# A one-layer bidirectional hybrid encoder: the norm factor broadcast as a stationary operand, and the last products and stores shared out differently

## The chip, the cores and the metric

One Trainium2 chip, one of its cores. A core has five engines with a queue each: TensorE (PE, matrix products), VectorE (DVE), ScalarE (ACT), GpSimd (POOL) and SyncE (SP, which here only issues DMAs; ACT's queue issues some as well). The metric is the device time of one execution in microseconds, as a median of several executions; lower is better. Everything is float32, one sequence of 512 tokens, 1024 channels.

## The reference

```python
def _rmsnorm(x, w):
    xf = x.astype(jnp.float32)
    y = xf * lax.rsqrt(jnp.mean(xf * xf, axis=-1, keepdims=True) + EPS)
    return (y * w.astype(jnp.float32)).astype(x.dtype)

def _modulate(x, shift, scale):
    return x * (1.0 + scale) + shift

def reference(x, c, ...):
    h = x
    c_act = jax.nn.silu(c)
    mod = c_act @ w_ada + b_ada
    sh1, sc1, g1, sh2, sc2, g2, sh3, sc3, g3 = jnp.split(mod, 9, axis=-1)
    u = _modulate(_rmsnorm(h, norm_ffn1), sh1, sc1)
    h = h + 0.5 * g1 * _swiglu(u, w_ffn1_up, w_ffn1_down)
    u = _modulate(_rmsnorm(h, norm_mix), sh2, sc2)
    h = h + g2 * _hybrid_mixer(u, ...)
    u = _modulate(_rmsnorm(h, norm_ffn2), sh3, sc3)
    h = h + 0.5 * g3 * _swiglu(u, w_ffn2_up, w_ffn2_down)
    return _rmsnorm(h, norm_final)
```

The two feed-forward nets have 2816 inner channels. The mixer projects `u` to 7712 columns, and has a gated short convolution (branch A) and a bidirectional gated DeltaNet of 8 heads (branch B): five-tap convolutions of q, k and v, per-head decays, a chunked delta-rule scan in each direction, a gated norm. Both branches are projected, merged by gates and projected once more. What this change touches is the RMSNorm: four times the factor `rsqrt(mean(x*x) + EPS)` of each token is needed on all channels, and the last time the result is the output.

## The kernel before

Channels lie on the 128 partitions and tokens along the rows: `h` is 8 tiles of 128 x 512. A weight tile of 512 KB is loaded by SP (L167, tile `raw`), split into two exact parts by ACT (L172, `hi`) and DVE (L174, `lo`), and each product is three matmuls, L184 to L186. PE does these nearly all the time.

The sum over channels for a norm crosses partitions, so PE does it: the squares are summed over the tiles on DVE (L208), and `rstd_bcast` (L211 to L233) multiplies them as the stationary operand by a column of ones (L218, L221), which gives 128 sums, one per partition and token. DVE turns them into means (L223, `ms`), POOL raises them to the power -1/2 (L226, `rs`, one column for every 128 tokens). To bring the factor of a token onto all partitions, DVE makes a diagonal matrix of each column (L229, `diag`), and PE multiplies ones by it (L232): each row of the result holds the factors of all tokens. The function runs seven times: once for 512 tokens at the start (into the PSUM bank `kq`), and at the end of each feed-forward net and of the mixer twice, for the tokens 0 to 255 (`kq`) and 256 to 511 (`o`). Those six come from `residual` (L251), which gives the last product tile in two halves of the tokens, adds the residual (L256) and starts what follows on the first half.

At the start (L887 to L925) DVE computes the modulation from `w_ada` by products with an accumulator (L147, output `junk`), and each tile of `h` times the factor (L913 on DVE, L911 on POOL) goes through ACT (L915) to `u` and PE (L917). At the end `final` (L968 to L973) multiplies each tile of `h` by its norm weight and the factor, one DVE instruction per tile (L970), and stores tiles in pairs, alternately by SP's and ACT's queue (L973).

In the mixer eight heads are built one after the other. A head's decays come back from DRAM as `Gb` (L467), 128 x 8 x 128 on every partition, in a single buffer: the next head's load waits for this head's last readers (L526). DVE reads it at L512 and L514, ACT takes exponentials (L515), and DVE forms `ef` and `eb` (L526). Then PE multiplies k by k and q (L545, L546), and DVE scales the results (L550, L554). ACT's L482 takes sums of squares of what PE has transposed (L477).

The order of tasks in the mixer comes from a hand-written list, EMIT. Beyond that, the instructions of each engine stand in an order that a scheduler makes from the program's order, priorities (`high_priority`) and its own costs. Each engine then runs its queue strictly in that order, waiting wherever an operand or a buffer is missing. So a changed instruction can move others far away from it.

## Time and profile before

| What | Value |
|---|---|
| Median of 3 runs | 1392.18 us (1391.95 to 1394.26) |
| Profiled execution, span | 1388.2 us |
| PE busy | 1342.6 us, 97% |
| DVE busy | 824.8 us, 59% |
| ACT busy | 565.6 us, 41% |
| POOL busy | 71.9 us, 5% |
| Last matmul of the down products starts | 1376.26 us |
| Last store is issued | 1384.6 us |

Of the profiled execution only the span, first to last instruction, is known; the times of the runs are some 4 us above it. A line of the timeline reads: start in us, duration, engine, line of the program, operation, output and inputs, shapes, count, and in brackets the time that the engine was idle before it with what it waited for last. A row such as "PE acc L917 <- ACT u L915: 6.9, 6, 2.2" says who waited for whom: total us, how often, the longest. A row that begins with two times and a colon is a stretch: its length, the busy time (and count) of PE, of PE's weight loads, of DVE, ACT and POOL, the granted clock of PE as a share of full speed, the busy share of the DMA engines and GB/s. SPq and ACTq are DMA issues on these queues.

### The profile page before, as it was taken

How to read it: one execution, taken by the hardware profiler on the slowest of the kernel's cores; microseconds unless marked ns; L12 is line 12 of the kernel's file. 1: busy time of each engine (PE TensorE's matmuls, PEld its weight loads, DVE VectorE, ACT ScalarE, POOL GpSimd, SP SyncE). 2: the span in 40 equal slices, each digit the busy share in tenths (PEclk: the TensorE clock that was granted, in tenths of full speed). 3: DMA queues.
4: the chain of work that ended last, by engine and by line, in shares of the span. 5: the costliest groups of instructions: out<-in, count | busy, mean ns of one | idle time of the engine just before them, and what ended most of it. 6: DMA issues, size and time to landing. Idle time of an engine off the chain costs nothing.

```text
span 1388.2 us, 19980 instructions
## 1 busy us (share of the span) xinstructions
PE 1342.6 (97%) x7359; PEld 1101.4 (79%) x7359; DVE 824.8 (59%) x2199; ACT 565.6 (41%) x1156; POOL 71.9 (5%) x109
## 2 busy tenths in 40 slices
PE   5999999999999999999999999999999999999997
PEld 2588888888897777878787787888898888888886
DVE  7856655655566778787764784647653444443343
ACT  3433333322346654467645333545433333332230
POOL 2000000000010110021112001000000000000000
PEclk9999999999999999999999999999999999999998
DMA  8655555645532446334342333567503333332331
GB/s 278 220 173 182 177 188 167 193 158 190 173 126 71 123 122 154 125 92 131 113 139 73 113 112 100 161 197 253 177 31 106 122 112 131 122 115 86 99 110 61
DMA packets 88131, 193.50 MB, mean 139 GB/s; under 512 B 24737, under 2 KB 37217, under 8 KB 87906
## 3 DMA queue, kind: packets, MB, share of 16 engines
q1 hardware_dynamic: 72400, 163.77, 38.1%
q10 hardware_dynamic: 15634, 28.46, 5.9%
q8 instruction: 58, 0.95, 0.3%
q14 instruction: 39, 0.32, 0.1%
HBM read 171.19 MB, written 21.00 MB: 138 GB/s over the span
## 4 chain that ended last, share of the span: by engine, by line
PE 80%; DMA 7%; DVE 6%; issue 4%; ACT 3%; POOL 1%; ACTq 0%; POOLq 0%; DVEq 0%; SPq 0%
PE acc L186 23%; PE acc L185 23%; PE acc L184 23%; DMA Gb<-grow 2%; DMA msb<-gtd 2%; DVE junk L147 1%; DVE lo L174 1%; PE ch L672 1%; DMA raw<-w_o 1%; PE ch L683 1%; PE o L695 1%; PE tp L477 1%; PE tp L608 1%; PE ch L700 1%; ACT hi L172 1%
## 5 line engine op out<-in xcount | busy, mean ns | idle before, releaser
L185 PE MATMUL acc<-uh,lo 128*128 128x512 f32 (+1 forms) x1256 | 486.2, 387 | 1.3 <-DVE lo L174 1.3
L184 PE MATMUL acc<-uh,hi 128*128 128x512 f32 (+1 forms) x1256 | 486.4, 387 | 0.7 <-ACT hi L172 0.6
L186 PE MATMUL acc<-ul,hi 128*128 128x512 f32 (+1 forms) x1256 | 485.2, 387 | 0.0
L172 ACT CAST hi<-raw 128x512 fp32r<-128x512 f32 (+1 forms) x424 | 257.5, 613 | 540.4 <-PE acc L186 481.5
L174 DVE TENSOR_TENSOR lo<-raw,hi 128x512 fp32r<-128x512 f32 (+1 forms) x424 | 286.4, 681 | 282.7 <-ACT hi L172 281.5
L185 PEld LDWEIGHTS acc<-uh,lo 128*128 128x128 f32 x1256 | 237.3, 189 | 44.5 <-DVE lo L174 1.8
L184 PEld LDWEIGHTS acc<-uh,hi 128*128 128x128 f32 x1256 | 237.2, 189 | 44.4 <-ACT hi L172 1.0
L186 PEld LDWEIGHTS acc<-ul,hi 128*128 128x128 f32 x1256 | 236.9, 189 | 42.7
L147 DVE SCALAR_TENSOR_TENSOR junk<-raw,cs 128x256 f32<-128x256 f32 x288 | 111.3, 437 | 60.3 <-DMA raw<-w_ada 60.1
L184 PE MATMUL acc<-gh,hi 128*128 128x512 f32 (+1 forms) x396 | 145.1, 366 | 0.0
L186 PE MATMUL acc<-gl,hi 128*128 128x512 f32 (+1 forms) x396 | 145.1, 366 | 0.0
L185 PE MATMUL acc<-gh,lo 128*128 128x512 f32 (+1 forms) x396 | 144.7, 365 | 0.0
L184 PEld LDWEIGHTS acc<-gh,hi 128*128 128x128 f32 x396 | 74.7, 189 | 12.2
L185 PEld LDWEIGHTS acc<-gh,lo 128*128 128x128 f32 x396 | 74.7, 189 | 12.0
L186 PEld LDWEIGHTS acc<-gl,hi 128*128 128x128 f32 x396 | 74.7, 189 | 12.0
L442 DVE SCALAR_TENSOR_TENSOR cacc<-acc,cvd_sb,cacc 128x510 f32<-128x510 f32 (+1 forms) x96 | 71.1, 743 | 7.5 <-ACT cacc L437 6.9
L311 DVE TENSOR_TENSOR sa<-sa,acc 128x512 f32<-128x512 f32 x42 | 28.8, 686 | 35.3 <-PE acc L186 35.3
L226 POOL TENSOR_TENSOR rs<-ms,mhalf 128x2 f32<-128x2 f32 (+1 forms) x7 | 5.7, 813 | 830.4 <-DVE ms L223 817.5
L194 ACT CAST gh<-sa 128x512 fp32r<-128x512 f32 x44 | 27.4, 622 | 23.7 <-DVE sa L311 18.5
L204 ACT ACTIVATE sq<-h 128x512 f32<-128x512 f32 (+1 forms) x25 | 14.1, 563 | 46.5 <-DVE h L256 46.3
L195 DVE TENSOR_TENSOR gl<-sa,gh 128x512 fp32r<-128x512 f32 x44 | 30.5, 692 | 3.3 <-ACT gh L194 1.4
L917 PE MATMUL acc<-u,lw 128*128 128x512 f32 x48 | 25.3, 667 | 6.9 <-ACT u L915 6.9
(242 smaller groups left out, 1399.5 us busy)
## 6 DMA issues: line engine op xcount, KB each, us to landing
raw<-w_ada SPq DMA_DIRECT2D x72, 512.0 KB
raw<-w_in SPq DMA_DIRECT2D x60, 512.0 KB
raw<-w2u SPq DMA_DIRECT2D x44, 512.0 KB
raw<-w1u SPq DMA_DIRECT2D x40, 512.0 KB
raw<-w1d SPq DMA_DIRECT2D x16, 512.0 KB
raw<-w2d SPq DMA_DIRECT2D x16, 512.0 KB
Gb<-grow SPq DMA_DIRECT2D x8, 512.0 KB
dl<-nl SPq DMA_DIRECT2D x8, 512.0 KB
```

What stands on the lines that cost most here:

```text
L147: dve.scalar_tensor_tensor(out=junk[:], in0=raw[:, q, :], scalar=1.0, in1=cs[:, q, :], op0=ALU.mult, op1=ALU.mult, accum_out=part[:, n, q ...
L172: act.copy(hi[:], raw[:, k : k + n, :])
L174: dve.tensor_sub(lo[:], raw[:, k : k + n, :], hi[:].bitcast(F32))
L184: pe.matmul(ps[:, t0:t1], wh, rh[:, k0 + k, t0:t1], start=a, stop=False)
L185: pe.matmul(ps[:, t0:t1], wl, rh[:, k0 + k, t0:t1], start=False, stop=False)
L186: pe.matmul(ps[:, t0:t1], wh, rl[:, k0 + k, t0:t1], start=False, stop=b)
L194: act.copy(hi, src)
L195: dve.tensor_sub(lo, src, hi.bitcast(F32))
L204: act.activation(out=sq[:], in_=hk, func=ACT.Square)
L311: dve.tensor_mul(sa[:], sa[:], ps[1][:])
L442: dve.scalar_tensor_tensor(out=acc[:, lo:hi], in0=src[:, lo + o : hi + o], scalar=w[:, i : i + 1], in1=acc[:, lo:hi], op0=ALU.mult, op1=AL ...
L917: pe.matmul(early[m][:], lw[:, m, k, :], u0[:], start=k == 0, stop=k == KT - 1)
```

## The change

In `rstd_bcast` the diagonal matrices are gone, and so is the product of ones with them. For each 128 tokens PE multiplies with a stationary operand that is the column `rs` repeated 128 times (read with a stride of zero) and the identity as the moving operand: the result holds again the factors of all tokens on each partition. DVE has sixteen instructions less, and PE has n matmuls of 128 columns in place of one of n x 128.

In `final`, for tokens 256 to 511 only, ACT copies the factor from PSUM to SBUF (`bs`); for tiles 0, 1 and 2 ACT multiplies `h` by the norm weight, which needs no factor, and POOL multiplies the result by `bs`; the other five tiles go through DVE as before. Each tile is stored by itself, tiles 0, 2, 4 and 6 by SP's queue, the others by ACT's. The first half of the tokens is treated as before.

```diff
     def rstd_bcast(sums, t0, t1, tag):
...
         rs = sm["p"].tile([P, NC], F32, tag="rs", name="rs")
         pool.tensor_tensor(out=rs[:, 0:n], in0=ms[:, 0:n], in1=mhalf[:, 0:n], op=ALU.pow)
-        diag = sm["p"].tile([P, n, P], F32, tag="sq", name="diag")
+        bc = bank(tag, psx)
         for i in range(n):
-            dve.tensor_scalar(out=diag[:, i, :], in0=ident[:], scalar1=rs[:, i : i + 1], scalar2=None,
-                              op0=ALU.mult)
-        bc = bank(tag, psx)
-        pe.matmul(bc[:, 0 : t1 - t0], ones[:], diag[:].rearrange("p a b -> p (a b)"), start=True, stop=True)
+            pe.matmul(bc[:, i * P : i * P + P], rs[:, i : i + 1].to_broadcast([P, P]), ident[:], start=True, stop=True)
         return bc
...
     def final(t0, t1, bc):
+        n = t1 - t0
+        some = (0, 1, 2) if t1 == T else ()
+        if some:
+            bs = sm["p"].tile([P, n], F32, tag="bs", bufs=1, name="bs")
+            act.copy(bs[:], bc[:, 0:n])
         for k in range(KT):
-            dve.scalar_tensor_tensor(out=h[:, k, t0:t1], in0=h[:, k, t0:t1], scalar=nw[:, 3, k : k + 1],
-                                     in1=bc[:, 0 : t1 - t0], op0=ALU.mult, op1=ALU.mult)
-            if k % 2:
+            hk = h[:, k, t0:t1]
+            if k in some:
+                act.activation(out=hk, in_=hk, func=ACT.Copy, scale=nw[:, 3, k : k + 1])
+                pool.tensor_tensor(out=hk, in0=hk, in1=bs[:], op=ALU.mult)
+            else:
+                dve.scalar_tensor_tensor(out=hk, in0=hk, scalar=nw[:, 3, k : k + 1], in1=bc[:, 0:n], op0=ALU.mult,
+                                         op1=ALU.mult)
+            if some:
+                (nc.sync, nc.scalar)[k % 2].dma_start(out[:, k, t0:t1], hk)
+            elif k % 2:
                 (nc.sync, nc.scalar)[k // 2 % 2].dma_start(out[:, k - 1 : k + 1, t0:t1], h[:, k - 1 : k + 1, t0:t1])
```

The scheduler gives another order, above all at the start, at the boundary to the mixer and in the mixer. Three places are shown; lines of the new kernel stand some four lower in the mixer (L463 there is L467 above, L508 is L512, L510 is L514, L438 is L442, L546 is L550, L550 is L554, L562 is L566, L568 is L572).

SP's DMA issues in the mixer around the load of `Gb` for the fourth head, before (`dl` and `A` are the way of the inverses' blocks to DRAM and back, `raw` a weight tile):

```order
L566 DMA dl<-nl 128x1024
L572 DMA A<-dl 8x32x32
L167 DMA raw<-w_in 128x1024
L572 DMA A<-dl 8x32x32 x2
L167 DMA raw<-w_in 128x1024
L572 DMA A<-dl 8x32x32
L167 DMA raw<-w_in 128x1024
L572 DMA A<-dl 8x32x32
L566 DMA dl<-nl 128x1024
L467 DMA Gb<-grow 128x8x128
```

and now:

```order
L562 DMA dl<-nl 128x1024
L167 DMA raw<-w_in 128x1024
L463 DMA Gb<-grow 128x8x128
L568 DMA A<-dl 8x32x32 x2
L167 DMA raw<-w_in 128x1024
L568 DMA A<-dl 8x32x32
L167 DMA raw<-w_in 128x1024
L568 DMA A<-dl 8x32x32
L562 DMA dl<-nl 128x1024
```

The load of `Gb` stood behind two further weight tiles and the next `dl`; now it stands right behind the first of these weight tiles.

DVE at the readers of that `Gb`, before:

```order
L554 TENSOR_TENSOR at<-o,ef 128x256
L554 TENSOR_TENSOR at<-o,eb 128x256
L442 SCALAR_TENSOR_TENSOR cacc<-acc,cvd_sb,cacc 128x510
L442 SCALAR_TENSOR_TENSOR cacc<-acc,cvd_sb,cacc 128x511
L174 TENSOR_TENSOR lo<-raw,hi 128x512
L442 SCALAR_TENSOR_TENSOR cacc<-acc,cvd_sb,cacc 128x511
L442 SCALAR_TENSOR_TENSOR cacc<-acc,cvd_sb,cacc 128x510
L174 TENSOR_TENSOR lo<-raw,hi 128x512
L512 TENSOR_TENSOR st<-Gb,G 128x4
L514 COPY st<-Gb 128x4
```

and now:

```order
L514 TENSOR_TENSOR st<-st 128x4
L174 TENSOR_TENSOR lo<-raw,hi 128x512
L438 SCALAR_TENSOR_TENSOR cacc<-acc,cvd_sb,cacc 128x510
L438 SCALAR_TENSOR_TENSOR cacc<-acc,cvd_sb,cacc 128x511
L508 TENSOR_TENSOR st<-Gb,G 128x4
L510 COPY st<-Gb 128x4
L438 SCALAR_TENSOR_TENSOR cacc<-acc,cvd_sb,cacc 128x511
L174 TENSOR_TENSOR lo<-raw,hi 128x512
L438 SCALAR_TENSOR_TENSOR cacc<-acc,cvd_sb,cacc 128x510
L508 TENSOR_TENSOR st<-Gb,G 128x4
L510 COPY st<-Gb 128x4
L174 TENSOR_TENSOR lo<-raw,hi 128x512
```

The readers stood behind both `at` of the head before and behind six further weight splits; now they stand ahead of these (the `nl` and `at` of the head before follow later), between two weight splits.

DVE at the start, before:

```order
L223 TENSOR_SCALAR ms<-tp 128x4
L147 SCALAR_TENSOR_TENSOR junk,part<-raw,cs 128x256
L229 TENSOR_SCALAR diag<-ident,rs 128x128 x4
L147 SCALAR_TENSOR_TENSOR junk,part<-raw,cs 128x256 x6
L151 TENSOR_REDUCE mod<-part 128x2
L152 TENSOR_TENSOR mod<-mod,b_sb 128x2
L155 SCALAR_TENSOR_TENSOR ga<-mod,nw 128x1
L913 TENSOR_TENSOR t<-h,kq 128x512
L147 SCALAR_TENSOR_TENSOR junk,part<-raw,cs 128x256 x8
L913 TENSOR_TENSOR t<-h,kq 128x512
```

and now:

```order
L223 TENSOR_SCALAR ms<-tp 128x4
L147 SCALAR_TENSOR_TENSOR junk,part<-raw,cs 128x256 x7
L151 TENSOR_REDUCE mod<-part 128x2
L152 TENSOR_TENSOR mod<-mod,b_sb 128x2
L155 SCALAR_TENSOR_TENSOR ga<-mod,nw 128x1
L909 TENSOR_TENSOR t<-h,kq 128x512 x2
L147 SCALAR_TENSOR_TENSOR junk,part<-raw,cs 128x256 x8
```

The four `diag` are gone between the first `junk` and the next, and the second `t` stands ahead of eight `junk` instead of behind them.

More of the change, by code (lines that the diff above doesn't have):

```diff
@@ L269, in residual @@
             ww = [(weight(w, nk, lead["p"]), k0, nk, f, l) for w, k0, nk, f, l in ws(m)]
-            held.append((m, ww, [bank()] * 2 if tail > 1 else [bank(), bank()], res(m)))
+            held.append((m, ww, [bank()] * 2 if tail > 1 else [bank() for _ in HALVES], res(m)))
         def half(i):
@@ L275, in half @@
                     yield from product_steps(ps[i], w, rhs, k0, nk, f, l, *HALVES[i][:2])
-        todo = [half(0), half(1)]
         for i, (t0, t1, tag) in enumerate(HALVES):
-            for _ in todo[i]:
+            for _ in half(i):
                 pass
```

## The prediction

> **What bounds the kernel now.** I read the page first, then the waits of TensorE (PE), then the timeline around the places where the order of instructions changes.
>
> ```profile
> PE 1342.6 (97%) x7359; PEld 1101.4 (79%) x7359; DVE 824.8 (59%) x2199; ACT 565.6 (41%) x1156; POOL 71.9 (5%) x109
> PEclk9999999999999999999999999999999999999998
> PE acc L917 <- ACT u L915: 6.9, 6, 2.2
> PE o L545 <- DVE at L554: 4.1, 3, 3.5
> PE kq L232 <- DVE diag L229: 3.6, 4, 2.4
> PE tp L477 <- ACT junk L482: 3.1, 1, 3.1
> PE o L232 <- DVE diag L229: 2.1, 2, 1.6
> ```
>
> PE is busy 97% of 1388.2 us (45.6 us are not), so a microsecond counts only where PE waits, at the end behind PE's last matmul, or at the start ahead of its steady work. The rows below are PE's waits: releaser, total us, times, longest. Those that the edit touches by name are the two on `diag`: 5.7 us in six waits, of which 2.4 lie at the start and 1.6 at the end. All other waits it can touch only through the order.
>
> The profiled execution spans 1388.2 us and the median of the runs is 1392.18, so 4.0 us lie around the span; the sum below is made against the span and the 4.0 us are put back at the end. About 0.2% (2.8 us) is what a measurement of this kernel can tell from no change.
>
> **The end.** This is the one place where both parts of the change work together, and nothing hides it.
>
> ```profile
> 1378.80 0.70 POOL L226 TENSOR_TENSOR rs<-ms,mhalf 128x2 f32<-128x2 f32 x1 [9.39 <-DVE ms L223]
> 1379.53 0.48 DVE L229 TENSOR_SCALAR diag<-ident,rs 128x128 f32<-128x128 f32 x2 [0.88 <-POOL rs L226]
> 1380.06 0.50 PEld L232 LDWEIGHTS o<-diag,ones 128*128 128x128 f32 x2 [1.69 <-DVE diag L229]
> 1380.07 1.22 PE L232 MATMUL o<-diag,ones 128*128 128x256 f32 x2 [1.61 <-DVE diag L229]
> 1381.33 3.22 DVE L970 SCALAR_TENSOR_TENSOR h<-h,nw,o 128x256 f32<-128x256 f32 x8 [1.32 <-PE o L232]
> 1382.22 1.94 SPq L973 DMA_DIRECT2D out<-h  x2
> L973 ACTq DMA_DIRECT2D out<-h x4: 378/384/398, 1372.4 to 1384.6; - x4
> L911 POOL TENSOR_TENSOR t<-h,bs 128x512 f32<-128x512 f32 x6 | 8.4, 1411 | 15.9 <-ACT u L915 12.1 <-ACT bs L892 3.7
> L645 POOL TENSOR_TENSOR nl<-t,st 64x256 f32<-64x256 f32 x8 | 5.4, 678 | 39.8 <-ACT t L620 39.8
> ```
>
> Rows one, two, four and five are a chain, one engine after the other: `rs` ends at 1379.50, `diag` at 1380.01, the factor `o` at 1381.29, the eight products at 1384.55, 0.40 each (3.22 / 8). The last store is issued at 1384.6 (second number of the last range in the row of the ACT queue), and the span ends 3.6 later.
>
> After the change: `diag` goes, 1379.53 to 1380.07, 0.54 us. Its two instructions are replaced by none on DVE; PE's one matmul of 256 columns (two passes, 1.22) becomes two of 128 columns, again 256 columns twice, so I take 1.22: `o` is there at 1380.8. Whether a stationary operand read with stride zero loads slower no row shows; bounds: no dearer (the passes are the same), or one more load exposed for each of the four passes (0.25, half of the 0.50 of the two in the weight-load row). DVE then has five products, 5 × 0.40 = 2.0, done at 1382.8. ACT copies `o` to `bs`: 128x512 took 0.58 at the start (row below), so 256 columns about 0.4: `bs` at 1381.2. POOL's three products: half of 1411 ns for 128x512 is 0.71, and 64x256 took 0.68; I take 0.70: done at 1381.9, 1382.6 and 1383.3. The pre-multiplication on ACT lies in the last token half's down products, where ACT has 59% idle time over the span; at nothing, and about 0.4 each if the cover were gone.
>
> The last product is thus 1.2 earlier (1383.3 against 1384.55), but the stores do not follow at once. SP issues tiles 0, 2, 4, 6 in this order, ACT 1, 3, 5, 7. Tile 2 is POOL's last, so 4 and 6, which DVE has long finished, stand behind it: issues at 1383.3, 1383.7 and 1384.1, at 0.38 each. The last issue is 0.5 earlier, not 1.2, and each store carries half as much. **Term: −0.7**, between −0.2 (POOL 0.15 dearer a product) and −1.5 (the halved store gives back more).
>
> One row could speak against POOL: at the start its three products ran beside DVE work with two operands in SBUF, and that work took 1.48 rather than 0.42 (rows below), while DVE's `t<-h,kq`, one operand in PSUM, took 0.69 beside POOL. The products at the end have `h` in SBUF and `o` in PSUM, like the latter, so I add nothing. The Trainium skill, page "SBUF — State Buffer", section "Who interferes with whom", states that a DVE instruction with at most one SBUF input stays off the port pair it shares with GpSimd, while one with two SBUF inputs blocks against GpSimd's reads; by this rule too nothing is added, and if it failed here three DVE products at 1.48 would take the whole gain.
>
> **The start.** Here DVE, not PE, is the bound.
>
> ```profile
> 14.36 1.05 POOL L226 TENSOR_TENSOR rs<-ms,mhalf 128x4 f32<-128x4 f32 x1 [12.97 <-DMA cva_sb<-cva]
> 15.44 0.87 DVE L229 TENSOR_SCALAR diag<-ident,rs 128x128 f32<-128x128 f32 x4 [0.90 <-POOL rs L226]
> 16.23 0.42 DVE L147 SCALAR_TENSOR_TENSOR junk<-raw,cs 128x256 f32<-128x256 f32 x1
> 16.37 2.07 PE L232 MATMUL kq<-diag,ones 128*128 128x512 f32 x2 [2.37 <-DVE diag L229]
> 18.48 0.58 ACT L892 COPY bs<-kq 128x512 f32<-128x512 f32 x1 [7.54 <-PE kq L232]
> 19.10 0.69 DVE L913 TENSOR_TENSOR t<-h,kq 128x512 f32<-128x512 f32 x1
> 20.62 1.48 DVE L147 SCALAR_TENSOR_TENSOR junk<-raw,cs 128x256 f32<-128x256 f32 x1
> 21.00:54.00 33.00, 28.31 (x57) 10.93 (x56) 32.05 (x141) 10.89 (x17) 6.52 (x5) 1.00 0.78 264
> ```
>
> In the last row (us, then busy time of PE, its weight loads, DVE, ACT, POOL) DVE has 32.05 of 33 us, and PE's 6.9 us of waits for `u` come through it. `diag` costs DVE 0.90 idle and 0.87 busy, 1.77 in all; without it DVE goes straight on with `junk`. `kq` can then be there at 15.45 + 2.07 = 17.5 instead of 18.4, and DVE, which needs it after seven `junk`s and three small instructions, does not wait for it. The whole 1.77 comes back only if the chain through ACT's `u` and PE's L917 follows; the new order also puts the second `t<-h,kq` ahead of eight `junk`s. **Term: −1.2**, between 0 (the weight tiles' DMAs, at 264 GB/s, set the pace after all) and −1.8.
>
> **The four factors in between** (first feed-forward to mixer, mixer to second feed-forward, first half of the end). PE's waits on `diag` there are 5.7 − 2.4 − 1.6 = 1.7. Each shrinks by at most the 0.48 of a `diag`; against that the scheduler has put other DVE work ahead of six weight splits at the first boundary, some 0.2 to 0.5. **Term: −0.5**, between −1.7 and +0.5.
>
> **The mixer's order.** Its computation is the same, but the scheduler has moved its instructions. Two places decide.
>
> ```profile
> 438.93 0.39 SPq L467 DMA_DIRECT2D Gb<-grow  x1
> 447.74 0.17 DVE L512 TENSOR_TENSOR st<-Gb,G 128x4 f32<-128x4 f32 x1 [4.38 <-DMA Gb<-grow]
> 451.18 1.12 PE L477 MATMUL tp<-ident,cacc 128*128 128x128 f32 x4 [3.11 <-ACT junk L482]
> 452.00:454.00 2.00, 2.00 (x7) 1.62 (x6) 1.56 (x2) 1.99 (x3) 0.36 (x1) 0.50 0.31 84
> 456.00:458.00 2.00, 2.00 (x11) 1.64 (x10) 0.74 (x1) 0.00 (x0) 0.00 (x0) 0.77 0.65 147
> 1003.40 0.35 PE L218 MATMUL tp<-ones,ssum 128*128 128x1 f32 x2 [2.11 <-DVE ssum L208]
> 1004.00:1006.00 2.00, 2.00 (x19) 2.00 (x19) 0.16 (x1) 0.17 (x1) 0.22 (x1) 1.00 0.20 70
> ```
>
> First stall: head 0's decay matrix `Gb` takes 8.8 us from issue (438.93) to DVE's use (447.74); DVE waits 4.38, ACT's Exp stands behind it, and PE waits 3.11 for ACT. The granted clock, 1.00 before, is then 0.50 until about 456.9 (the 0.77 of 456 to 458 is half speed for 0.9 us): 5.7 us at half speed, 2.9 us lost beside the 3.11. In the new order the decays' PE work stands about 0.9 us of PE time earlier, and PE's stall where it was; so `Gb` comes up to 0.9 earlier, unless `hsave`'s 2 MB, also issued earlier, slow the loads. I take the stall 0.3 shorter and the clock as before. **Term: −0.3**, between −3.5 and +1.0: a wait of 2.11 us (1003.40) left the clock at 1.00, so a stall cut to 2.2 may save the slow stretch with it. The Trainium skill, page "TensorE: Matmul & The Clock Gate", section "What's actually happening", has the clock fall to half after an idle window of about 3.4 us that runs free of the program; by it a stall of either length may or may not drop the clock, depending on where it falls.
>
> ```profile
> L442 DVE SCALAR_TENSOR_TENSOR cacc<-acc,cvd_sb,cacc 128x510 f32<-128x510 f32 (+1 forms) x96 | 71.1, 743 | 7.5 <-ACT cacc L437 6.9
> 497.50 0.47 DVE L526 TENSOR_SCALAR eb<-Gb,G 128x128 f32<-128x128 f32 x2
> 506.94 0.68 DVE L174 TENSOR_TENSOR lo<-raw,hi 128x512 fp32r<-128x512 f32 x1
> 508.33 0.39 PE L185 MATMUL acc<-uh,lo 128*128 128x512 f32 x1
> 509.01 0.38 PE L545 MATMUL o<-kT 128*128 128x128 f32 x2
> 513.23 0.34 DVE L550 SCALAR_TENSOR_TENSOR nl<-o,st,eb 128x128 f32<-128x128 f32 x1
> 514.00 0.43 SPq L467 DMA_DIRECT2D Gb<-grow  x1
> 524.26 0.17 DVE L512 TENSOR_TENSOR st<-Gb,G 128x4 f32<-128x4 f32 x1 [5.50 <-DMA Gb<-grow]
> 526.87 0.50 PE L185 MATMUL acc<-uh,lo 128*128 128x512 f32 x1 [0.99 <-DVE lo L174]
> ```
>
> Second place, 497 to 530: `Gb` has one buffer; its last readers L526 end at 497.97, yet the next load is issued only at 514.00, since it stands late in SP's order. DVE waits 5.50 for it, late, and PE loses 0.99. In the new order this load stands seven SP issues earlier, so it goes out at about 498.9 (L526 end some 0.9 later there) and lands 8.8 to 10.3 us on (438.93 to 447.74, and 514.00 to 524.26), at 507.7 to 509.2. But its reader L512 is moved too, ahead of the weight split that ran at 506.94 and whose result PE uses at 508.33, and ahead of the L550 and L554 that release PE's next L545. With L512, one copy, one L442 (0.74, first row) and the split itself (0.68), it ends at 509.4 to 510.7: PE waits 1.1 to 2.4. Behind it on DVE stand two more splits, five more L442 and four L550 before the two L554, some 7 us by the durations shown; they end at about 516, and PE, which reached its second L545 at 509.0 before and has 2.5 us more work ahead of it now, gets there at 512.6 to 513.9: a wait of up to 3. Gone is the 0.99. I take 1.7 for the split, 1.3 for L545 and −1.0: **term +2.0**, between 0 (`Gb` in time or DVE with slack) and +6 (both waits at their upper ends, or the clock drops once).
>
> **Sum.** −0.7 − 1.2 − 0.5 − 0.3 + 2.0 = −0.7: a span of 1387.5, and with 4.0 around it **1391.5 us**.
>
> **Rivals.** (a) *Faster by over 2.8*: the new SP order costs nothing, because `Gb` lands before DVE reaches L512. For it speaks that the load is issued 15 us earlier; against it that L512 is moved by as much. −0.7 − 2.0 = −2.7, 1389.5; where the first stall also stays short enough to keep the clock at 1.00, 2.9 more, 1386.6. (b) *Slower*: the wait for `Gb` at L512 becomes PE's wait. Price at its upper end +6.0 instead of +2.0: −2.7 + 6.0 = +3.3, 1395.5; a wait at L545 of more than 3 us, like the first stall's 3.11, would bring the slow clock, 2.9 more, 1398. It decides from a landing later than 510. (c) *The end gives nothing*: POOL's products at 1.05 each (its `rs` of only 4 columns took that) end at 1384.4 and SP's three late stores at 1385.2; the end is 0.6 later instead of 0.7 earlier, 1392.8: inside no change.
>
> **How the numbers follow.** Between (a) and (b) lies the sum, with (c) inside it. Forecast with (c) 0.54; (a) 0.28; (b) 0.18. The range reaches down to (a) with the full clock, but for the last tenths, and up to (b) without the slow clock, **1386.8 to 1395.8**; beyond its ends I leave 0.2; the likeliest case alone 1389.4 to 1394.9. Faster by over 0.2% 0.28, within 0.54, slower 0.18.
>
> **What would show it.** Right: DVE without `diag`; at the start `kq` about 0.9 earlier and L917's last group a microsecond earlier; at the end the last store's issue at about 0.5 ahead of its distance now, with tiles 4 and 6 waiting on SP; around 505 to 510 a DVE wait L512 <- DMA `Gb`, and PE waits on `lo` L174 or on L554 that were not there. Wrong: a clock at 1.00 through the first stall; no wait on `Gb` around 508; POOL products far from 0.7.

## The result: slower by 0.22%, and outside the predicted range

The changed kernel took 1397.03 us (median of 20 runs, 1392.00 to 1400.41), the kernel before 1392.16 us (20 runs, 1389.06 to 1399.35). The ratio is 1.0022, with a 95% interval of 1.0012 to 1.0033: slower by 1.7 to 4.6 us. (The ratio is not formed from the two medians, which lie 4.9 us apart.) The prediction was 1391.5 us with a range up to 1395.8, and its likeliest case was no change. The mechanism of its rival (b), slower because the wait for `Gb` becomes a wait of PE, is what the profile shows.

The profiled execution spans 1397.3 us and is one of the longer of its kernel (its time was 1399.09, so 1.8 us lie around the span, not the 4.0 that I took for before). The profiled execution of before, 1388.2, was one of the shorter. So most of the 9.1 us between the two profiles is not the change: the executions of one kernel differ by 8 to 10 us among themselves, and the mean granted clock differs with them (in the changed kernel 0.989 for the longest execution, 0.993 for the shortest). I therefore compare stages, and take the clock out where it matters.

PE's waits in the changed kernel, in the view that the prediction showed of before (releaser, total us, times, longest; lines of the mixer stand four lower, so L541 was L545, L473 was L477):

```profile
PE o L541 <- DVE at L550: 7.7, 4, 4.1
PE acc L913 <- ACT u L911: 7.1, 6, 2.2
PE tp L473 <- ACT junk L478: 3.2, 1, 3.2
PE acc L185 <- DVE lo L174: 2.8, 3, 1.3
PE kq L229 <- POOL rs L226: 2.4, 4, 1.5
PE o L229 <- POOL rs L226: 1.1, 1, 1.1
PE acc L184 <- DVE sps L391: 0.9, 1, 0.9
```

and of before, the one of these rows that the prediction did not show:

```profile
PE acc L185 <- DVE lo L174: 1.3, 2, 1.0
```

The waits on `diag` (5.7 us) are gone and waits on `rs` stand in their place (3.5 us): 2.2 us less, as the edit says. But the wait of L541 for DVE's `at` has gone from 4.1 to 7.7 us, that of L185 for `lo` from 1.3 to 2.8, and one for `sps` is new.

The stretch behind the fourth load of `Gb`, timeline of the changed kernel (SP, DVE and PE rows picked in time order), and two stretches of its clock (length, busy time of PE, its loads, DVE, ACT, POOL, then granted clock):

```profile
501.52 0.37 SPq L463 DMA_DIRECT2D Gb<-grow  x1
511.03 0.17 DVE L508 TENSOR_TENSOR st<-Gb,G 128x4 f32<-128x4 f32 x1 [4.56 <-DMA Gb<-grow]
511.85 0.68 DVE L174 TENSOR_TENSOR lo<-raw,hi 128x512 fp32r<-128x512 f32 x1
512.58 0.50 PE L185 MATMUL acc<-uh,lo 128*128 128x512 f32 x1 [1.32 <-DVE lo L174]
518.11 0.41 DVE L550 TENSOR_TENSOR at<-o,ef 128x256 f32<-128x256 f32 x1
519.00 0.63 PE L541 MATMUL o<-kT 128*128 128x128 f32 x2 [2.91 <-DVE at L550]
489.00:496.00 7.00, 6.66 (x23) 5.72 (x24) 3.32 (x10) 2.15 (x7) 0.80 (x2) 0.55 0.47 142
519.00:523.00 4.00, 4.00 (x15) 3.52 (x16) 2.74 (x8) 1.88 (x4) 0.47 (x2) 0.57 0.46 151
```

This is the mechanism of rival (b) step by step: the load goes out early (12.5 us earlier than before's 514.00), takes 9.5 us to its reader, DVE waits 4.56 us for it with the weight split behind it, PE waits 1.32 for that split and then 2.91 at L541 for `at`. In this execution the clock is also at half speed for 3.4 us after the second wait (0.57 over these 4 us).

The end and the start of the changed kernel:

```profile
14.99 0.80 PE L229 MATMUL kq<-ident,rs 128*128 128x128 f32 x2 [1.46 <-POOL rs L226]
45.10 1.12 PE L913 MATMUL acc<-u,lw 128*128 128x512 f32 x2 [1.23 <-ACT u L911]
322.48 0.50 PE L185 MATMUL acc<-gh,lo 128*128 128x512 f32 x1 [1.13 <-DVE lo L174]
1389.07 0.81 PE L229 MATMUL o<-ident,rs 128*128 128x128 f32 x4 [1.10 <-POOL rs L226]
1389.91 0.37 ACT L970 COPY bs<-o 128x256 f32<-128x256 f32 x1 [2.83 <-PE o L229]
1390.32 2.05 DVE L977 SCALAR_TENSOR_TENSOR h<-h,nw,o 128x256 f32<-128x256 f32 x5 [2.08 <-ACT bs L970]
1390.36 2.09 POOL L975 TENSOR_TENSOR h<-h,bs 128x256 f32<-128x256 f32 x3 [1.35 <-ACT bs L970]
1391.11 2.68 SPq L980 DMA_DIRECT2D out<-h  x4
```

Two things here were not in the prediction: a wait at 322.48 that before does not have, and DVE's first product of the end, which starts only when ACT's copy `bs` has ended (1389.91 + 0.37), although both only read `o`. Whether the chip or the program's own dependencies order the two, no run shows.

### The profile page after: what moved, and what is told of

It reads as the page before. It is cut to its first block, busy times and chain, and to the rows that moved or that the text cites. A ratio compares the mean times of both kernels' runs of the same rounds, so it can differ in the third digit from the quotient of the medians.

```text
span 1397.3 us, 20010 instructions
## 1 busy us (share of the span) xinstructions
PE 1347.4 (96%) x7377; PEld 1106.3 (79%) x7377; DVE 819.5 (59%) x2180; ACT 570.7 (41%) x1162; POOL 74.3 (5%) x112
## 4 chain that ended last, share of the span: by engine, by line
PE 77%; DMA 8%; DVE 7%; issue 3%; ACT 3%; POOL 1%; ACTq 0%; POOLq 0%; SPq 0%; DVEq 0%
PE acc L186 22%; PE acc L184 22%; PE acc L185 22%; DMA msb<-gtd 2%; DMA Gb<-grow 2%; DMA raw<-w_ada 2%; DVE junk L147 1%; DVE lo L174 1%; PE ch L668 1%; DVE cacc L438 1%; DMA ybd<-z 1%; PE o L691 1%; PE ch L679 1%; PE tp L604 1%; PE tp L473 1%
## 5 line engine op out<-in xcount | busy, mean ns | idle before, releaser
L185 PE MATMUL acc<-uh,lo 128*128 128x512 f32 (+1 forms) x1256 | 487.0, 388 | 1.7 <-DVE lo L174 1.7
L185 PEld LDWEIGHTS acc<-uh,lo 128*128 128x128 f32 x1256 | 237.6, 189 | 45.2 <-DVE lo L174 2.3
L185 PE MATMUL acc<-gh,lo 128*128 128x512 f32 (+1 forms) x396 | 145.1, 366 | 1.1 <-DVE lo L174 1.1
L186 PE MATMUL acc<-gl,hi 128*128 128x512 f32 (+1 forms) x396 | 144.7, 365 | 0.0
L185 PEld LDWEIGHTS acc<-gh,lo 128*128 128x128 f32 x396 | 74.7, 189 | 13.8 <-DVE lo L174 1.8
L438 DVE SCALAR_TENSOR_TENSOR cacc<-acc,cvd_sb,cacc 128x510 f32<-128x510 f32 (+1 forms) x96 | 71.0, 742 | 4.3 <-ACT cacc L433 3.8
```

What stands on the lines that cost most here:

```text
L185: pe.matmul(ps[:, t0:t1], wl, rh[:, k0 + k, t0:t1], start=False, stop=False)
L186: pe.matmul(ps[:, t0:t1], wh, rl[:, k0 + k, t0:t1], start=False, stop=b)
L438: dve.scalar_tensor_tensor(out=acc[:, lo:hi], in0=src[:, lo + o : hi + o], scalar=w[:, i : i + 1], in1=acc[:, lo:hi], op0=ALU.mult, op1=AL ...
```

## The experiments

Theory A: the order around the fourth `Gb` costs the time. Theory B: the new end does. Theory C: the broadcast itself, or the order at the boundary to the mixer, does.

**One part alone.** The factor broadcast in all seven places, with the old end:

```diff
-        diag = sm["p"].tile([P, n, P], F32, tag="sq", name="diag")
-        for i in range(n):
-            dve.tensor_scalar(out=diag[:, i, :], ...)
-        pe.matmul(bc[:, 0 : t1 - t0], ones[:], diag[:]..., start=True, stop=True)
+        for i in range(n):
+            pe.matmul(bc[:, i * P : i * P + P], rs[:, i : i + 1].to_broadcast([P, P]), ident[:], ...)
```

> The change's first part alone (the factor broadcast as a stationary operand in all seven places); the end's products and stores as before. The mixer's order is then the changed kernel's. Theory A, the moved load and readers of the fourth head's decay matrix Gb cost PE: slower than before by 3 to 6 us, PE waits L185 <- DVE lo of 1 to 2.4 and L545's like <- DVE at of 2 to 3 near 512 and 519, as in the changed kernel. Theory B, the shared products and single stores at the end cost: within 1 us of before or faster by about 1.8 (the start).

1393.48 us against 1391.48, ratio 1.0017 (1.0002 to 1.0033): slower, though by 2.0 us in the medians where theory A expected 3 to 6. The waits near 512 and 519 are there (0.93 at 509.01, 2.92 at 515.44). Then the end alone, with `diag` kept:

```diff
     def final(t0, t1, bc):
+        some = (0, 1, 2) if t1 == T else ()
... (the rest of the new `final`, as above)
```

> The change's second part alone: POOL takes three of the last eight products, single-tile stores; the factor by diagonal matrices as before, so the mixer's order is that of before. Theory A: 0.2 to 1.0 us faster than before (the end's 0.4 in the two profiles), nothing else moves. Theory B: slower than before by 3 us or more, seen behind PE's last matmul.

1391.60 us, ratio 1.0000 (0.9983 to 1.0016). So the new end is not what costs (theory B falls), but it gains nothing either: the expected 0.2 to 1.0 us are not seen.

**The one factor that sets the order.** One of the seven calls sets the mixer's order: the second, the first token half at the boundary to the mixer. Both directions ran: the whole change but for this call, and before with this call alone changed. In the first the fourth load of `Gb` is issued at 514.32, late as before (514.00); in the second at 499.44, early as in the changed kernel (501.52).

```diff
+    DIAG = (2,)
...
+        calls.append(n)
+        if len(calls) in DIAG:
+            diag = sm["p"].tile([P, n, P], F32, tag="sq", name="diag")
...
+            pe.matmul(bc[:, 0 : t1 - t0], ones[:], diag[:].rearrange("p a b -> p (a b)"), start=True, stop=True)
+            return bc
```

> The whole change, except that the second of the seven factors (first token half, first feed-forward to mixer) keeps its diagonal matrix; the order around Gb is then that of before (load behind dl, readers behind both at). Theory A: the waits at 512 and 519 are gone, the 0.99 near 527 is back, and the time is 1 to 3 us below before, 4 to 7 below the changed kernel. Theory C, PE's broadcast matmuls or the general reordering cost: within 1.5 us of the changed kernel.

1390.59 us, ratio 0.9996 (0.9982 to 1.0010): the loss is gone, but a time 1 to 3 us below before is not shown.

```diff
+    CAST = (2,)
...
+        calls.append(n)
+        if len(calls) in CAST:
+            bc = bank(tag, psx)
+            for i in range(n):
+                pe.matmul(bc[:, i * P : i * P + P], rs[:, i : i + 1].to_broadcast([P, P]), ident[:], start=True, stop=True)
+            return bc
```

> Before, except that the second of the seven factors alone is broadcast as a stationary operand. Two matmuls in place of two DVE instructions and one matmul, and the order around Gb of the changed kernel. Theory A: slower than before by 4 to 7 us (the changed kernel without the gains of start and end). Theory C: within 1 us of before.

1395.45 us, ratio 1.0027 (1.0012 to 1.0043): 4.0 us slower by the medians, at the lower end of theory A's 4 to 7. PE's waits in this second kernel, which keeps `diag` in six of seven places and the old end:

```profile
487.73 0.77 PE L554 MATMUL o<-kT 128*128 128x128 f32 x2 [3.92 <-DVE at L563]
510.83 0.50 PE L185 MATMUL acc<-uh,lo 128*128 128x512 f32 x1 [1.42 <-DVE lo L174]
517.25 0.76 PE L554 MATMUL o<-kT 128*128 128x128 f32 x2 [2.91 <-DVE at L563]
```

and in the first, which is the changed kernel but for two DVE instructions:

```profile
486.98 0.77 PE L553 MATMUL o<-kT 128*128 128x128 f32 x2 [3.21 <-DVE at L562]
527.03 0.50 PE L184 MATMUL acc<-uh,hi 128*128 128x512 f32 x1 [1.23 <-ACT hi L172]
528.53 0.50 PE L185 MATMUL acc<-uh,lo 128*128 128x512 f32 x1 [0.99 <-DVE lo L174]
```

The pair of waits comes and goes with this one call. The two DVE instructions that were saved here are worth half a microsecond; the order that comes with their absence costs some 3 to 4. This shows that the order is to blame, not yet which part of it, since both the boundary and the stretch around `Gb` move.

**Only the `Gb` order undone.** All seven factors are broadcast, and the four small instructions that read the second head's `Gb` (two lines, once for each direction) get a slightly lower priority. That puts the fourth load and its readers back to their old places (the load is issued at 511.46) and leaves the boundary as it is in the changed kernel: PE's instructions are the same up to 489 us, DVE's up to 448. The changed kernel ran again beside it.

```diff
+                with tc.high_priority(-5 if hd == 1 else 0):
                     for d in range(2):
                         last = (P - 1, 0)[d]
                         dve.tensor_sub(wj[...], Gb[...], G[:, d, :, hd])
                         dve.tensor_copy(el[...], Gb[...])
```

> The whole change, all seven factors broadcast, and one thing more: the two instructions that read the second head's Gb get a priority lower by 5. That alone gives SP and DVE around the fourth head's Gb the order that they had before (load at row 172 of SP, readers behind the 163rd weight split), and moves 10 rows of PE. Theory A (the place of the fourth Gb and its readers costs): no waits on lo and at near 512 and 519, time 1 to 3 us below before and 4 to 7 below the changed kernel, as with the diagonal kept in the second factor. Theory C (the broadcast at the boundary to the mixer itself, or its order there, costs): still 3 to 6 us slower than before.

> The changed kernel once more, beside its variants on one chip. Theory A and C alike: 3 to 5 us slower than before; PE waits of 1 to 1.5 near 512 and 2.9 near 519.

The changed kernel: 1395.30 us, ratio 1.0024 (1.0009 to 1.0039), as before. With the `Gb` order undone: 1393.09 us, ratio 1.0010 (0.9990 to 1.0029); theory A expected it 1 to 3 us below before and theory C 3 to 6 above, so both missed. Its waits show why:

```profile
485.61 0.46 PE L542 MATMUL o<-kT 128*128 128x128 f32 x2 [2.52 <-DVE at L551]
506.38 0.46 PE L542 MATMUL o<-kT 128*128 128x128 f32 x2 [0.96 <-DVE at L551]
523.33 0.49 PE L184 MATMUL acc<-uh,hi 128*128 128x512 f32 x1 [0.38 <-ACT hi L172]
524.82 0.50 PE L185 MATMUL acc<-uh,lo 128*128 128x512 f32 x1 [1.00 <-DVE lo L174]
```

The 1.32 and the 2.91 are gone, and 0.96, 0.38 and 1.00 have come. And the boundary's own loss is still there. Stage lengths from the profiles show where the loss stands. The boundary runs from the end of the second `rs` to the first transposes (L477, where the first stall ends); the `Gb` stretch runs from there to the last L545 wait near 600, less what the granted clock took from PE's work (from a table of the clock in steps of 1 us). One profile stands behind each number:

| Kernels | boundary, us | `Gb` stretch at full clock, us |
|---|---|---|
| order of before: before, end alone, start alone, second factor's `diag` kept | 60.2, 60.5, 60.6, 60.9 | 140.7, 141.4, 141.2, 141.7 |
| order of the change: changed, again, broadcast alone, second factor alone, the two variants of the end | 61.4, 61.5, 61.3, 61.2, 61.4, 62.6 | 144.5, 144.3, 144.3, 144.8, 144.1, 144.7 |
| `Gb` order undone | 61.9 | 142.7 |

The boundary costs about 0.9 us more and the `Gb` stretch 3.2 more. Something comes back behind them: from there to the fourth `rs`, the one that ends the mixer's first token half, it takes 410.3 to 412.0 us at full clock in the four profiles with the order of before and 409.1 to 410.5 in the six with the changed one, about 1.0 less. At the boundary PE waits at 424.88 in the changed kernel:

```profile
424.08 0.65 DVE L438 SCALAR_TENSOR_TENSOR cacc<-acc,cvd_sb,cacc 128x510 f32<-128x510 f32 x1
424.64 0.22 DVE L391 TENSOR_TENSOR sps<-sps,spe 128x64 f32<-128x64 f32 x1
424.88 0.47 PE L184 MATMUL acc<-uh,hi 128*128 128x512 f32 x1 [0.93 <-DVE sps L391]
```

This wait, 0.93 each time, is in all nine profiles with the changed order at the boundary and in none of the five with the old one. The decays' small instructions now stand among the convolution taps that read PE's accumulators. PE's product does not read `sps`; I read the wait as PE waiting for the bank that the tap at 424.08 still reads, which no run shows (the tap ends at 424.73, `sps` at 424.86, PE starts at 424.88). By where it stands, some three quarters of the loss are theory A's, and the rest theory C's in the form "the order at the boundary". By what the undoing gives back the share is smaller and loose: 1.8 of the 3.2 us in one profile, with other waits in place of the two.

**The start.** Before, with only the first factor broadcast:

> Before, with only the first of the seven factors (the start) broadcast as a stationary operand; the mixer's order is that of before but for some rows at the start. Theory A, with the start's gain given back later: the start's last wait L917 <- u comes 1.35 us earlier against the first matmul of the norm sums (33.4 us after it rather than 34.8), and a wait of PE for lo L174 of 0.8 to 1.6 us appears near 322, where DVE waits for a tile of w_ada; the time is within 1 us of before. Rival: the wait at 322 comes from the mixer boundary's order and is absent here; 1.0 to 1.5 us faster.

1391.35 us, ratio 0.9995 (0.9980 to 1.0010). The start is shorter by the 1.35 us expected (the L917 wait of 1.97 stands at 36.14, 24.62 after the first norm sum's matmul at 11.52; the changed kernel has the same distance, before has 1.34 more), and the wait near 322 appears, smaller than expected:

```profile
321.71 0.50 PE L185 MATMUL acc<-gh,lo 128*128 128x512 f32 x1 [0.52 <-DVE lo L174]
```

In nine other profiles with the new start it is 0.6 to 1.9 us, in none of four with the old start does it exist. What PE waits for there is a weight split that stands in DVE's order behind `junk` products, and those wait for a tile of `w_ada`. In before that wait ended at 319.83, in the changed kernel at 320.35, though the tile's load was issued 1.1 us earlier there (314.10 rather than 315.24):

```profile
319.83 0.43 DVE L147 SCALAR_TENSOR_TENSOR junk<-raw,cs 128x256 f32<-128x256 f32 x1 [2.30 <-DMA raw<-w_ada]
```

```profile
320.35 0.42 DVE L147 SCALAR_TENSOR_TENSOR junk<-raw,cs 128x256 f32<-128x256 f32 x1 [4.64 <-DMA raw<-w_ada]
```

The first row is before, the second the changed kernel: PE was 1.8 us earlier (0.5 of it by the inputs' DMAs), but the tile came no earlier. The changed kernel's DMA packets show what was late. In the first row below, of 316.9 to 318.3, queue 8, which carries the program's own instructions, moves one packet of 16 KB (columns: packets, MB, share of the 16 DMA engines); it takes 0.97 us, from 317.14. The second row is the stretch before DVE goes on, and the DMA engines carry hardly anything in it (last two columns: 0.04 busy, 14 GB/s):

```profile
q8 instruction: 1, 0.02, 4.4%
318.60:320.30 1.70, 1.70 (x10) 1.39 (x9) 0.00 (x0) 0.46 (x1) 0.00 (x0) 1.00 0.04 14
```

The trace has sixteen landing events for this load: fifteen lie before 318.59, the last at 320.26. In before the last two came at 319.68 and 319.73. In all ten profiles with the new start the last event is 1.3 to 1.8 us behind the fifteenth, and an instruction packet runs while the tile is moving; in the four with the old start it is 0.13 us or less behind, and the packet begins in the last 0.6 us of the tile. I read this as the packet holding up one sixteenth of the tile. Which DMA engine carried it is not recorded.

From the first norm sum to the end of the second `rs` it takes 378.8 to 379.2 us in four profiles with the old start and 378.3 to 379.4 in nine with the new one (381.2 in one more, where the clock fell near 324): hardly anything of the start's gain reaches the mixer. With the first factor alone broadcast the wait is short, and some 0.5 us of the gain are left at that point, too little for the times to show.

**The end.** One execution each: all eight products on DVE with single-tile stores, and POOL's three kept but the stores in the order in which products end.

```diff
-        some = (0, 1, 2) if t1 == T else ()
+        some = ()
...
-            if some:
+            if t1 == T:
                 (nc.sync, nc.scalar)[k % 2].dma_start(out[:, k, t0:t1], hk)
```

> The changed kernel with all eight last products on DVE again, no copy to bs, still stored tile by tile. In the changed kernel DVE's first product waits for ACT's copy of the factor (0.4 us) and SP's stores of tiles 4 and 6 stand behind POOL's tile 2. If these two use up the gain, the time from the last norm sum's first matmul (L221 <- sq) to the end is 9.9 to 10.2 us here, against 10.2 to 10.8 in the runs of the changed end; if not, 10.6 or more.

```diff
-            if some:
-                (nc.sync, nc.scalar)[k % 2].dma_start(out[:, k, t0:t1], hk)
-            elif k % 2:
+            if not some and k % 2:
...
+        for i, k in enumerate((3, 4, 5, 0, 6, 1, 7, 2) if some else ()):
+            (nc.sync, nc.scalar)[i % 2].dma_start(out[:, k, t0:t1], h[:, k, t0:t1])
```

> The changed kernel with the eight last stores issued in the order in which the products end (3, 4, 5, 0, 6, 1, 7, 2, alternately SP and ACT). If the stores behind POOL's tile 2 cost what I say, the last issue comes right after the last product and the time from L221 <- sq to the end falls by 0.5 to 0.9 us against the changed kernel's 10.2 to 10.8. If the end is set otherwise, it stays.

From PE's first L221 of the last half to the end of the span it takes 9.00 us with all on DVE and 9.73 with the reordered stores. The changed end takes 10.16, 10.48, 10.56, 10.63 and 10.78 in five profiles with the broadcast and 10.78 in the one with `diag`; the old end takes 10.13 to 10.57 in four profiles with `diag` and 10.05 in the one with the broadcast. So the new end is not shorter than the old one with either form of the factor. The first variant falls even below what was expected, the second by what was expected, but not for the reason that I gave. The last issue does not set the end: the span ends 3.1 to 4.2 us after it. Over 14 profiles the span ends 5.8 to 6.4 us after the **first** store of the last half is issued, whatever their number and size: before 5.98 (issue at 1382.22), all on DVE 5.82, stores reordered 5.93, changed 6.19. Two stretches behind this first issue show why, of before and of the kernel with all on DVE (last two columns: busy share of the DMA engines, GB/s):

```profile
1383.10:1385.70 2.60, 0.00 (x0) 0.00 (x0) 1.45 (x4) 0.00 (x0) 0.00 (x0) 0.50 0.97 325
1387.10:1389.60 2.50, 0.00 (x0) 0.00 (x0) 1.50 (x4) 0.00 (x0) 0.00 (x0) 0.50 0.99 333
```

About 1 us after the first issue the DMA engines are fully busy with the 1 MB, and they stay so for some 3 us, until about 2 us ahead of the end. Later issues only have to keep them fed. In the changed kernel they are not fed so well at first (189 GB/s from 1392.3 to 1393.3), and the end comes 6.19 behind the first issue. What moves the end most is how soon that first one goes.

```profile
1384.62 0.71 PE L229 MATMUL o<-ident,rs 128*128 128x128 f32 x4 [1.10 <-POOL rs L226]
1385.37 3.22 DVE L977 SCALAR_TENSOR_TENSOR h<-h,nw,o 128x256 f32<-128x256 f32 x8 [1.58 <-PE o L229]
1385.88 2.68 SPq L980 DMA_DIRECT2D out<-h  x4
```

Here, in the kernel with all on DVE, the first store is issued 0.51 us after DVE starts, right behind one product. In the changed kernel it waits for ACT's copy (0.4) and for POOL's 0.70, because tiles 0 and 1, the first on both queues, are POOL's; before, it waited for a pair of products. Part of the 9.00 is clock: `o` took 0.71 at full clock here, and 0.81 to 1.22 in the other profiles with the broadcast. Behind `o`, where that plays no part, the first store goes 0.69 us sooner than in the changed kernel. The reordered stores appear in a second profile, with `Gb` by heads (below): 9.93 us, against 10.56 without them at the same clock of `o`.

**What the stalls hang on.** If `Gb`'s 9 us from issue to use cause the stalls, a faster load must remove them, in both kernels. The load reads 512-byte rows, eight for each partition, because heads alternate in DRAM. With the rows of one head side by side it is one piece of 4 KB for each partition:

```diff
+            Gp = dt.tile([P, H, 2 * NC], F32, name="Gp")
...
-            pe.transpose(ps[0:64, 0:P], G[:].rearrange("p d c h -> p (d c h)"), ident[:])
+            act.copy(Gp[:], G[:].rearrange("p d c h -> p h (d c)"))
+            pe.transpose(ps[0:64, 0:P], Gp[:].rearrange("p h a -> p (h a)"), ident[:])
-            grow = scr.tile([2 * NC, H, P], F32, tag="grow", name="grow")
+            grow = scr.tile([H, 2 * NC, P], F32, tag="grow", name="grow")
... (the store to `grow` alike)
-                nc.sync.dma_start(Gb[:], grow[:, hd, :].unsqueeze(0).to_broadcast([P, 8, P]))
+                nc.sync.dma_start(Gb[:], grow[hd].unsqueeze(0).to_broadcast([P, 8, P]))
```

> The changed kernel with the decay rows kept in DRAM head by head, so that a head's Gb is read in pieces of 4 KB rather than 512 bytes (one more ACT copy of 128x64 orders them); other mixer order, with the fourth Gb's readers behind the 164th weight split. If the time from Gb's issue to its use (8.8 to 10 us) is what the first two stalls of the mixer hang on, it falls to 4 to 6 us, the stalls of 3.2 and 4.1 shrink by 2 to 4 each and the slow clock behind them goes: 5 to 10 us below the changed kernel. If Gb's time does not depend on the pieces: stalls as before, and 1 to 3 us below before, by the order alone.

> The kernel before with the same change of Gb's rows and nothing else. If Gb's time is what the stalls hang on: 4 to 8 us below before. If not: within 1.5 us of before.

On the changed kernel: 1386.08 us, ratio 0.9966 (0.9950 to 0.9983). On before: 1386.57 us, ratio 0.9968 (0.9954 to 0.9982). Both lie where they were expected if `Gb`'s time is what the stalls hang on: 9.2 us below the changed kernel and 4.4 below before. Issue and use of the first `Gb` in the changed kernel with this load:

```profile
440.58 0.34 SPq L465 DMA_DIRECT2D Gb<-grow  x1
444.86 0.17 DVE L510 TENSOR_TENSOR st<-Gb,G 128x4 f32<-128x4 f32 x1 [0.94 <-DMA Gb<-grow]
```

It takes 4.3 us instead of 9.1 (8.8 in before), and DVE's waits on `Gb` fall from 13.9 us to 0.9 (in before from 13.9 to 2.3). The stalls of 3.2 and 4.1 us are 0 and 0.36, the pair at 512 and 519 is one wait of 0.50. The new layout moves the mixer's order too, so not each tenth is the load's; but both kernels gain, and the medians are but 0.5 us apart (1386.08 and 1386.57). At full clock (the table below) 1.6 of some 4 us between them remain. They fit the boundary, which with this load takes 60.2 us in the changed kernel and 58.3 in before; the former has waits of 0.93 for `sps` and 0.73 for a copy of ACT there, the latter none. So the `Gb` loads cost the larger part and the order at the boundary the smaller, and this pair of runs shows it better than the undoing above. Last, this with the reordered stores:

> The changed kernel with Gb's rows kept head by head in DRAM, and the last stores in the order in which the products end. No stalls on Gb, end 0.5 to 0.9 us shorter: 5 to 6 us faster than before. If only Gb counts: 4.5 to 5 us faster.

1386.20 us, ratio 0.9948 (0.9932 to 0.9965): 0.52% faster than before. Whether the reordered stores add to the gain, the times do not tell: 1386.08 without them, on another chip.

**Time at full clock.** Span times mean granted clock of each execution, averaged, tells the kernels apart better than medians: among the executions of before the spread (standard deviation) falls from 2.2 to 2.4 us to 1.1 to 1.3. It is rough, since waits do not follow the clock. The standard errors are 0.2 to 0.5 us. Each kernel has to be compared with before on its own chip: the first value of before goes with both parts alone, the second factor alone and its `diag` kept, the second with the changed kernel again, the `Gb` order undone and `Gb` by heads, the third with the start alone and the reordered stores; the changed kernel's 20 have none beside them.

| Kernel | executions | mean clock | span x clock, us |
|---|---|---|---|
| before, beside three sets | 35, 30, 17 | 0.992, 0.992, 0.992 | 1379.3, 1378.9, 1379.9 |
| changed; again | 20; 12 | 0.992; 0.993 | 1383.5; 1383.4 |
| broadcast alone | 12 | 0.993 | 1383.2 |
| second factor alone | 12 | 0.991 | 1382.1 |
| `Gb` order undone | 12 | 0.994 | 1382.7 |
| end alone | 12 | 0.992 | 1379.9 |
| start alone | 12 | 0.993 | 1380.0 |
| second factor's `diag` kept | 12 | 0.993 | 1379.9 |
| `Gb` by heads: on the change; on before; with stores reordered | 7; 12; 6 | 0.994; 0.993; 0.994 | 1376.5; 1374.9; 1376.4 |

The changed kernel costs some 4 us (4.5 beside before on the same chip), and not by the clock, whose mean is the same. By this table the gains of start and end cannot be told from nothing, and neither can the change but for the second factor. Two numbers stay open. The stages of the profiles add up to about 3.1 (0.9 + 3.2 − 1.0), so about 1 us of the loss has no place in this account. And with the `Gb` order undone 1382.7 is 0.7 below the changed kernel, where its profile shows 1.8 less in the `Gb` stretch; one profile against twelve executions does not decide that.

## Why the prediction was wrong, step by step

**The end, forecast −0.7, measured 0 or a little more.** `o` came 0.5 us earlier, DVE's products took 0.41 each and POOL's 0.70, as reckoned, and nothing collided with POOL. Two steps failed. DVE "then has five products" at once: it waited for ACT's copy, 0.41 us, and before's own rows showed this, since at the start `t<-h,kq` begins at 19.10 when ACT's `bs` of the same bank has ended at 19.06. And "The last store is issued at 1384.6 ..., and the span ends 3.6 later" took the last issue for what sets the end; it is the first, 6 us ahead, and in the changed kernel that one waits for the copy and for POOL.

**The start, forecast −1.2, measured −1.35 there and 0 in the end.** The local term was right. "comes back only if the chain ... follows" went no further than PE's L917; the gain is given back 270 us later, at a tile of `w_ada` whose last part comes late. I had named the weight tiles' DMAs as what could take this term to 0, but within the start, and by their rate; a collision with an instruction packet was not in it.

**The four factors in between, forecast −0.5, measured +1.2 at the boundary to the mixer.** The waits on `diag` did go. The step that failed is "some 0.2 to 0.5" for the new DVE order at the boundary: I priced the splits that stand later, not the wait of 0.93 behind the decays' instructions, which now stand among the taps. From the end of the second `rs` to the beginning of the first stall it takes 57.1 to 57.5 us with the old order and 58.1 to 58.6 in five of the seven profiles with the new one (58.7 and 59.3 in the others). The two later boundaries show nothing: from the fourth to the sixth `rs` it takes 362.6 to 363.0 us at full clock with either order.

**The first stall, forecast −0.3, measured −0.3.** It is 2.8 to 3.3 us with the new order (3.0 in the mean of seven) and 3.1 to 3.5 with the old (3.3 in the mean of four), so the boundary as a whole is the 0.9 of the table. The clock fell after it in some executions and not in others of the same kernel. The traces show why. In each of the 14 profiles every change of the granted clock lies a whole number of 3.413 us from every other, so the clock is decided in windows of that length, and where they begin differs from execution to execution. Two executions of the changed kernel, in their own windows (length, busy time of PE, its loads, DVE, ACT, POOL, then granted clock):

```profile
447.47:450.88 3.41, 1.35 (x6) 0.77 (x5) 2.26 (x13) 1.62 (x7) 0.00 (x0) 1.00 0.28 114
450.89:454.30 3.41, 2.25 (x8) 1.96 (x9) 3.34 (x5) 3.38 (x9) 0.64 (x1) 0.50 0.26 58
447.70:451.11 3.41, 1.56 (x7) 0.94 (x6) 2.40 (x13) 1.76 (x7) 0.00 (x0) 1.00 0.26 105
451.12:454.52 3.40, 2.38 (x13) 2.04 (x14) 3.33 (x5) 3.37 (x9) 0.64 (x1) 1.00 0.24 65
```

The stall of 3.23 is cut by the window's end into 2.07 and 1.16, and half clock follows; the stall of 2.88 into 1.86 and 1.02, and the clock stays. Over the 14 profiles, between 30 and 1370 us, half clock followed all 24 windows at full clock in which PE was idle for 1.97 us or more by the profile, 11 of 135 with 0.7 to 1.96, and none with less. The rule of the Trainium skill that I cited ("TensorE: Matmul & The Clock Gate", section "What's actually happening") has the clock fall to half after an idle window of about 3.4 us that runs free of the program. The traces agree on the window and that it runs free, but 2 us of idle time within it were enough here. So "a stall cut to 2.2 may save the slow stretch" was a matter of luck: what counts is how the window cuts the stall.

**The `Gb` stretch, forecast +2.0 with 0 to +6, measured +3.2.** The mechanism was right in every link, and the waits of 1.32 and 2.91 lie within "1.1 to 2.4" and "up to 3". Mis-sized was what I took, the wait at L545 above all: 1.7 + 1.3 − 1.0, where 1.3 + 2.9 − 1.0 was measured. (That this sum meets the stretch's 3.2 to the tenth is luck; the second stall, for one, is longer by 0.4 in the mean.) I had computed "up to 3" for L545 and taken less than half of it, though the very rows gave PE's and DVE's arrival and their difference.

**The sum** was −0.7. With what was measured its terms are 0 + 0 + 1.2 − 0.3 + 3.2 = +4.1. That is near the executions' 4, but in part by chance, since the gain of about 1.0 in the rest of the mixer, which the sum did not have, is not in it. So the end and the start failed as terms, since their gains (1.9 us together) did not last, and the boundary and the wait at L545 failed in size. The 4.0 "around the span" was misread but did no harm: 1.8 lie around it, and the other 2.2 are what that execution lay below the median, so adding 4.0 gave the median of before again (1392.2).

**The rivals.** (b) came true in its mechanism, with 0.18 of the chance. Its price of +3.3 fits the measured 4 in part by luck: it put the `Gb` stretch at +6.0 and the other terms at −2.7, where 3.2 and about +0.9 were measured. (a) failed because L512 moved as far as its load. (c) was wrong in its price (POOL took 0.70, not 1.05), though right in that the end gave nothing.

## What to carry to other kernels

Where a scheduler or a planner orders the engines, a small edit is first of all a new order: find the place at which a transfer with a single buffer meets its reader, reckon both arrivals, and put the difference into the sum rather than the middle of a range. A gain at an early stage is only a gain if nothing behind it takes it back; follow it to the next wait on a DMA. And before an end is shared out among engines, see what the stores wait for: here the first store sets the end, and in the one execution of it eight products on one engine beat five and three on two.

## What the runs showed of the hardware that I had not expected

- Executions of one program on one core differ by up to 10 us (before: 1389.06 to 1399.35), and more than half of that goes with the granted clock (0.988 to 0.997 over all kernels). The clock falls to half for 3.4 us or 6.8 us at a time. After stalls of about 3 us in the mixer it took 1.5 to 3.1 us from PE's work, or nothing: behind the first 15 us the profile of the `Gb`-undone kernel lost 0.5 us to the clock, that of the second-factor kernel 9.5.
- What decides is PE's idle time within windows of 3.413 us that run on through the execution: 1.97 us or more were followed by half clock each time.
- A 512 KB load to all partitions took 8.7 to 11.6 us from issue to use in rows of 512 bytes (33 loads that DVE waited for), and 4.3 to 6.2 in rows of 4 KB (four such loads).
- The last of a tile's sixteen landing events came 1.3 to 1.8 us behind the fifteenth where a 16 KB packet of the program's instructions ran while it was moving (ten profiles).
- Stores of 1 MB in 4 or 8 pieces ended the span 5.8 to 6.4 us after the first issue, with the DMA engines 97% and 99% busy for 2.5 us of it in the two profiles shown.
- A 128x128 float32 product with a stationary operand read with stride zero costs what the plain one does: four passes in 0.71 at full clock, as many columns in two passes 0.70.
